# Second block of a transformer step: attention output in tiles of its own, two buffers for the S5 output matrix, gate tiles on a pair of banks, sums moved from GpSimd to VectorE

## Chip, cores and metric

One of the eight cores of a Trainium2 chip runs the kernel. Its engines are TensorE (PE in the rows, its weight loads PEld), VectorE (DVE), ScalarE (ACT), GpSimd (POOL) and SyncE (SP), which here issues DMAs. The metric is the device time of one execution in microseconds; lower is better.

## What is computed

The reference is two blocks in a row over 1024 tokens of 1024 columns. The first (differential attention, a gated delta rule, mixture of experts) and the last part of the second (output matrix, feed-forward) are not touched. What the change touches is the middle of the second block:

```python
h = _rms(x, norm1_g[l])
proj = h @ w_in[l]
u, q, k, v, qi, ki, wi, gates = jnp.split(proj, IN_SPLITS, axis=-1)
y_ssm = _s5_branch(u, A_re[l], ...)
...
```

`_s5_branch` is a state-space layer: 32 groups with 64 complex states each, scanned over time, then gelu and a gated linear unit (glu). The other branch is attention in blocks of 128 queries, in which each query sees only its 256 best keys by an index score (top-k). Both results go through a projection to 1024 columns, are multiplied by a sigmoid gate of their own (the 2048 columns `gates`) and added.

## The kernel before

Products have float32 accuracy: each operand is split into a high half, rounded to a format that TensorE takes in one pass, and a low half, and three matmuls (high by high, high by low, low by high) make one product (`K.mm3`). ACT makes the high half with a copy, another engine the low one by subtracting (`K.split`, L65 high and L66 low; for weights L75 `wh` and L76 `wl`, there on the engine in `K.sub`, which is GpSimd from the selection on).

The order of instructions on each engine is set by the scheduler of the tile framework, which takes the program's order and its own estimate of times; so a change in one place moves instructions in others. Tiles of one name share a ring of buffers. PSUM has the rings `lg` (two buffers of two banks), `tp` (two of one), `pj` and `po` (one each).

`stage_attn` is written in this order: norm of the input (`stage_norm2`, L1634 to L1650); index scores and queries; `select` for pairs of query blocks, a binary search for the top-k threshold (L1760 to L1846: count what lies above a threshold, one half on DVE and one on ACT, L1767, then one-element operations such as L1785), which ends in the mask `madd` (L1846); `attend` for the blocks 0 to 7; eight units of S5 (`s5_states`, `s5_out`), one beside each of the eight pieces of attend 6 and 7; 16 gate tiles of two halves each; `attn_branch` for the first 512 tokens (c=0) and for the others (c=1); `glu`; `merge`.

- `attend`: scores into `lg`, add of the mask with the maximum (L1867), exponential on ACT (L1870), reciprocal (L1872), scaling (L1876 on DVE from block 6 on, L1874 on POOL before), transposes into `tp` (L1883), split into `aph` and `apl` (L65, L66), product with V into `po`. Its queries are split by `stack` (L1665 on ACT, L1666 `aq`).
- `s5_states`: a matmul with `s5wi` into `lg`, products with cosines and sines (L1558 to L1560), a sum on POOL (L1561), four scans (L1563), the same back (L1565 on POOL, L1566, L1567), a sum (L1570). `s5_out` multiplies by `s5m` and `s5wo` and ends in gelu (L1585).
- `gate_tile` projects 128 gate columns in two halves of 24 matmuls of 128x512 through `pj` and takes a tanh (L1920). `u_tile` and `gate_tile` fill PE between the other parts.
- `attn_branch` loads the attention output `yatd` from DRAM (L1938), splits it into a part of the tile that held the block's input (`K.hh[:, 4:8]`), so after the gates of those columns have read it, multiplies by the projection, and applies the gate (L1950).
- `merge` adds the two branches (L2010 product with the gate, L2011 sum, L2012 and L2013 the split of the result).

Of the kernel before, what the change touches and what calls it, by code (L numbers as in the profile page):

```python
# [1530 lines left out]
def s5_states(K, wk, i, e):  # L1531


    nc = K.nc
    V, P = nc.vector, nc.gpsimd
    lo, hi = slice(0, 64), slice(64, 128)
    T = [128, 4, 128]
    g0 = 4 * i
    gs = slice(g0, g0 + 4)
    wi, wo, u = (wk.tile(T, F32, name="s5" + n, bufs=b) for n, b in (("wi", 2), ("wo", 1), ("u", 2)))  # L1540
    m = wk.tile([128, 4, 240], F32, name="s5m", bufs=2)
    cs = wk.tile([128, 4, 256], F32, name="s5cs", bufs=2)
    nc.sync.dma_start(wi, K.s5i[:, gs])
    nc.sync.dma_start(u, K.uTd[:, :, gs].rearrange("t p g c -> (t p) g c"))
    p0 = K.s5p[:, gs]
    nc.sync.dma_start(cs, bass.AP(tensor=p0.tensor, offset=p0.offset, ap=[[0, 2], [32 * 256, 64], [1, 1024]]))

    k0 = K.s5k[0:16, gs]
    nc.sync.dma_start(m.rearrange("p g x -> p (g x)")[:, 0:848],
                      bass.AP(tensor=k0.tensor, offset=k0.offset, ap=[[16, 8], [32 * 240, 16], [1, 848]]))  # L1550
    nc.sync.dma_start(wo, K.s5o[:, gs])
    co, si = cs[:, :, 0:128], cs[:, :, 128:256]
    e = e.rearrange("p (g c) -> p g c", g=4)
    for g in range(4):
        K.mm(e[:, g], wi[:, g], u[:, g], g == 0, True)

    a, r, z, c = (wk.tile(T, F32, name="s5" + n) for n in "arzc")
    V.tensor_mul(a, e, co)  # L1558
    V.tensor_mul(r[lo], e[hi], si[hi])
    V.scalar_tensor_tensor(r[hi], e[lo], -1.0, si[lo], op0=ALU.mult, op1=ALU.mult)  # L1560
    P.tensor_add(a, a, r)  # L1561
    for g in range(4):
        V.tensor_tensor_scan(z[:, g], K.rho[:, g0 + g:g0 + g + 1].to_broadcast([128, 128]), a[:, g], 0.0,  # L1563
                             op0=ALU.mult, op1=ALU.add)
    P.tensor_mul(c, z, co)  # L1565
    V.scalar_tensor_tensor(r[lo], z[hi], -1.0, si[hi], op0=ALU.mult, op1=ALU.mult)  # L1566
    V.tensor_mul(r[hi], z[lo], si[lo])  # L1567
    s = wk.tile([128, 4, 129], F32, name="s5s")
    P.memset(s[:, :, 0:1], 0.0)
    V.tensor_add(s[:, :, 1:129], c, r)  # L1570
    return m, u, wo, s
# [46 lines left out]
def stage_norm2(K, hp, ps):  # L1618

    nc, I = K.nc, K.I  # L1620
    K.hh = hp.tile([128, 8, L], F32R, name="hh")
    K.hl = hp.tile([128, 8, L], F32R, name="hl")
    K.rs1 = K.cst.tile([128, 8], F32, name="rs1")
    with ExitStack() as s:
        wk = K.pool(s, "n2w", 2, side="right")
        fg = wk.tile([128, D], F32, name="fg", bufs=1)
        gg = wk.tile([128, D], F32, name="gg", bufs=1)
        nc.sync.dma_start(fg, I["final_g"].rearrange("(a n) -> a n", a=1).to_broadcast([128, D]))
        nc.sync.dma_start(gg, I["norm1_g_2"].to_broadcast([128, D]))
        nc.gpsimd.tensor_mul(gg, gg, fg)  # L1630
        for t in range(8):
            ts = slice(t * 128, (t + 1) * 128)
            x = wk.tile([128, D], F32, name="x", bufs=4)
            nc.sync.dma_start(x, K.xacc[ts])  # L1634
            ss = wk.tile([128, 4], F32, name="ss")
            xf = wk.tile([128, D], F32, name="xf", bufs=3)
            (nc.gpsimd if t % 2 else nc.vector).tensor_mul(xf, x, fg)
            jk = wk.tile([128, D], BF, name="jk", bufs=1)
            nc.scalar.activation(jk, x, AF.Square, accum_out=ss[:, 0:1])
            nc.scalar.activation(jk, xf, AF.Square, accum_out=ss[:, 1:2])  # L1640
            r1 = K.rs1[:, t:t + 1]
            K.rstd(wk, r1, ss[:, 0:1], 1, 1, 1.0 / D)
            nc.vector.tensor_scalar(ss[:, 1:2], ss[:, 1:2], r1, r1, op0=ALU.mult, op1=ALU.mult)
            K.rstd(wk, ss[:, 2:3], ss[:, 1:2], 1, 1, 1.0 / D)
            nc.vector.tensor_mul(ss[:, 3:4], ss[:, 2:3], r1)
            nc.vector.scalar_tensor_tensor(xf, x, ss[:, 3:4], gg, op0=ALU.mult, op1=ALU.mult)
            for k0 in (0, 4):
                tp = ps.tile([128, 4, 128], F32, name="tp")
                for k in range(4):
                    nc.tensor.transpose(tp[:, k], xf[:, (k0 + k) * 128:(k0 + k + 1) * 128], K.ident)  # L1650
                K.split(K.hh[:, k0:k0 + 4, ts], K.hl[:, k0:k0 + 4, ts], tp)
# [197 lines left out]
def attend(K, wk, ps, b):  # L1849
# [3 lines left out]
    qt = wk.tile([128, 4, 128], F32, name="aqt")  # L1853
    nc.sync.dma_start(qt, K.qsd[b])
    qs = wk.tile([128, 2, 4, 128], F32R, name="aq", bufs=1)
    stack(K, qs, qt, nc.gpsimd.tensor_sub)
    for hp in range(2):
        po = ps.tile([128, 2, 2, 128], F32, name="po", bufs=1)
        for pp in range(2):
# [49 lines left out]
        nc.sync.dma_start(K.uTd[7 - t, :, f * 8:f * 8 + 8].rearrange("p g c -> g p c"), o[:, t])  # L1909


def gate_tile(K, wk, ps, f):

    nc = K.nc
    w = hcols(K, 1476 + f * 128, 128)
    o = wk.tile([128, L], F32, name="uo")
    for c in range(2):
        cs = slice(c * 512, (c + 1) * 512)
        q = proj_T(K, ps, w, 0, 128, c * 512, 512)
        nc.scalar.activation(o[:, cs], q, AF.Tanh, scale=0.5)  # L1920
    nc.sync.dma_start(K.sgt[f], o)

# [5 lines left out]
    yield q[:, 512:1024]  # L1928


def attn_branch(K, wk, gk, tag, ps, c):

    nc = K.nc
    cs = slice(c * 512, (c + 1) * 512)
    h, l = K.hh[:, 4:8, cs], K.hl[:, 4:8, cs]
    for k0 in (0, 2):
        r = wk.tile([128, 2, 512], F32, name=tag)
        nc.sync.dma_start(r, K.yatd[:, k0:k0 + 2, cs])  # L1938
        K.split(h[:, k0:k0 + 2], l[:, k0:k0 + 2], r)
    for f0 in (4, 6, 0, 2) if c else range(0, 8, 2):  # L1940
        if c == 0 or f0 < 4:
            K.wpa[f0] = K.wblock(K.I["w_proj_attn_2"][0], f0 * 128, 256)
        hs, ls = K.wpa[f0]
        g = gk.tile([128, 2, 512], F32, name=tag if c == 0 else "g", bufs=2 + 2 * c)
        nc.sync.dma_start(g, K.sgt[8 + f0:10 + f0, :, cs].rearrange("f p n -> p f n"))
        for i, q in enumerate((pair if c else narrow)(ps)):
            m = slice(i * 128, (i + 1) * 128)
            for k in range(4):
                K.mm3(q, (hs[k][:, m], ls[k][:, m]), (h[:, k], l[:, k]), k == 0, k == 3)
            nc.vector.scalar_tensor_tensor(g[:, i], g[:, i], 1.0, q, op0=ALU.add, op1=ALU.mult)  # L1950
        nc.sync.dma_start(K.mad[f0:f0 + 2, :, cs].rearrange("f p n -> p f n"), g)
# [42 lines left out]
def merge(K, wk, ps, y):  # L1994

    nc = K.nc
    A, B = K.hh, K.hl
    for f0 in range(0, 8, 2):
        hs, ls = K.wblock(K.I["w_proj_ssm_2"][0], f0 * 128, 256)
        for f in range(f0, f0 + 2):  # L2000
            g = wk.tile([128, L], F32, name="g", bufs=4)
            a = wk.tile([128, L], F32, name="ma")
            nc.sync.dma_start(g, K.sgt[f])
            nc.sync.dma_start(a, K.mad[f])
            m = slice((f - f0) * 128, (f - f0 + 1) * 128)
            for c, q in enumerate(pair(ps)):
                cs = slice(c * 512, (c + 1) * 512)
                for k in range(4):
                    K.mm3(q, (hs[k][:, m], ls[k][:, m]), (y[:, 0, k, cs], y[:, 1, k, cs]), k == 0, k == 3)
                nc.vector.scalar_tensor_tensor(g[:, cs], g[:, cs], 1.0, q, op0=ALU.add, op1=ALU.mult)  # L2010
                (nc.gpsimd if f < 7 else nc.vector).tensor_add(g[:, cs], g[:, cs], a[:, cs])  # L2011
                nc.scalar.activation(A[:, f, cs], g[:, cs], AF.Copy, scale=0.5)  # L2012
                nc.vector.scalar_tensor_tensor(B[:, f, cs], g[:, cs], 0.5, A[:, f, cs].bitcast(F32), op0=ALU.mult,  # L2013
                                               op1=ALU.subtract)


def stage_attn(K, hp, ew, dr):
# [8 lines left out]
    with ExitStack() as s:  # L2026
# [9 lines left out]
        with ExitStack() as s1:  # L2036
# [19 lines left out]
            w = hcols(K, 512, 512)  # L2056
            for t in range(8):
                q_tile(K, wk, ps, w, t)
        K.sub = nc.gpsimd.tensor_sub
        K.wh = wh  # L2060
        ps = Tags(pl, pj=pj, po=K.pool(s, "b3o", 1, PSUM))
        K.pjb = 1
# [14 lines left out]
        with ExitStack() as sw:  # L2077
# [5 lines left out]
            for _ in chain(attend(K, wk, ps, 6), attend(K, wk, ps, 7)):  # L2083
                next(units)
            next(units)
        for f in list(range(8, 16)) + list(range(8)):
            gate_tile(K, fk, ps, f)
        K.wpa = {}
        attn_branch(K, fk, fk, "uo", ps, 0)
        sa.close()  # L2090
        sr.close()
        bk = K.pool(s, "brw", 2)
# [1 line left out]
        with ExitStack() as sy:  # L2094
            yp = K.pool(sy, "yap", 1, side="right")
            ya = yp.tile([128, 2, 4, L], F32R, name="ya")
            with ExitStack() as sg:
                gk = K.pool(sg, "glw", 2)
                attn_branch(K, bk, bk, "ma", ps, 1)
                glu(K, bk, gk, ps, ya)  # L2100
            merge(K, bk, ps, ya)
        K.wh = w5
        K.w5 = out2_units(K, range(4))
    K.pjb = None
    K.sub = nc.vector.tensor_sub

def out2_units(K, us):
    wv = K.I["w_out_2"][0].rearrange("(k p) n -> p k n", p=128)
# [402 lines left out]
```

## Time and profile before

| | us |
|---|---|
| median of 3 runs | 3227.82 |
| lowest, highest run | 3227.03, 3231.82 |
| profiled execution, its own time | 3231.41 |
| its span | 3229.7 |

The stages of the profiled execution that the text speaks of:

| stage | us from the span's start |
|---|---|
| norm, scores, queries | 1776.6 to 1870 |
| selection, with attend 0 to 5 | 1870 to 2189.8 |
| attend 6 and 7, S5, the last gates, attention c=0 | 2189.8 to 2384.1 |
| attention c=1 and glu | 2384.1 to 2432 |
| merge, start of the output matrix | 2432 to 2482.5 |

The page gives shares of the whole span. The table by stage and the waits inside a stage tell which engine ends it. A row of waits reads: who waited, for whom, us in total, times, longest.

### The profile page before, as it was taken

Reading aid. Unit: us, or ns where it says so; the run is one execution under the profiler, and the core shown is the slowest. Engines: PE = TensorE matmul, PEld = TensorE weight load, DVE = VectorE, ACT = ScalarE, POOL = GpSimd, SP = SyncE. Lnnn points to the kernel's source line nnn. Section 1 sums busy time; section 2 is a strip of 40 time slices with the busy share of each in tenths; the row PEclk is TensorE's granted clock in tenths of the full one; section 3 lists DMA queues with packets and bytes.
Section 4 is the critical chain, followed back from the end, with each engine's and each line's share of the span. In section 5 each row is a group of like instructions: output and inputs, shape, how many; then the busy total and the mean of one; then the engine's idle time right before and its main releaser. Section 6 shows DMA issues by size and latency. Waiting matters only on the chain. (4 is left out here: it accounts for less than half of the span.)

```text
span 3229.7 us, 45092 instructions
## 1 busy us (share of the span) xinstructions
PE 2900.7 (90%) x15573; PEld 2387.0 (74%) x15573; DVE 2445.2 (76%) x4878; ACT 1656.9 (51%) x3161; POOL 804.9 (25%) x719
## 2 busy tenths in 40 slices
PE   3987999889897969999999699897698999999999
PEld 1655888778786748887777577776576788888787
DVE  6787665998886499999988599985567586555675
ACT  4433455365665228887776577663433243333343
POOL 4376111154554521111101324332225000000000
PEclk7988999889998979999999799999899999999999
DMA  5545665535324559999997223224575323333732
GB/s 204 150 144 170 192 182 175 151 112 152 105 86 144 176 189 379 382 398 366 370 372 249 73 66 90 65 70 128 136 248 177 123 72 103 109 109 105 290 111 101
DMA packets 370783, 567.04 MB, mean 176 GB/s; under 512 B 73075, under 2 KB 208104, under 8 KB 370554
## 3 DMA queue, kind: packets, MB, share of 16 engines
q1 hardware_dynamic: 365946, 547.37, 50.1%
q0 software_dynamic: 4608, 16.78, 2.2%
q8 instruction: 123, 2.02, 0.3%
q14 instruction: 106, 0.87, 0.1%
HBM read 446.12 MB, written 117.95 MB: 175 GB/s over the span
## 5 line engine op out<-in xcount | busy, mean ns | idle before, releaser
L1221 DVE TENSOR_TENSOR wl<-wraw,wh 128x1024 fp32r<-128x1024 f32 x384 | 446.9, 1217 | 10.9 <-ACT wh L1220 10.4
L1220 ACT ACTIVATE wh<-wraw 128x1024 fp32r<-128x1024 f32 x384 | 391.6, 1060 | 80.4 <-PE pu L57 42.6
L57 PE MATMUL pj<-hh,wh 128*128 128x512 f32 (+1 forms) x768 | 300.9, 392 | 17.6 <-ACT uo L1920 8.5
L57 PE MATMUL pj<-hh,wl 128*128 128x512 f32 (+1 forms) x768 | 295.7, 387 | 1.5 <-POOL wl L76 1.5
L57 PE MATMUL pj<-hl,wh 128*128 128x512 f32 (+1 forms) x768 | 295.9, 386 | 0.0
L57 PEld LDWEIGHTS pj<-hh,wh 128*128 128x128 f32 x768 | 148.3, 193 | 53.2 <-ACT uo L1920 11.7
L57 PEld LDWEIGHTS pj<-hh,wl 128*128 128x128 f32 x768 | 147.8, 193 | 35.4 <-issue 6.8
L57 PE MATMUL pj<-wh,hh 128*128 128x512 f32 (+1 forms) x400 | 159.8, 400 | 12.8 <-DVE g L2010 8.2
L57 PEld LDWEIGHTS pj<-hl,wh 128*128 128x128 f32 x768 | 148.2, 193 | 28.7 <-issue 3.8
L76 POOL TENSOR_TENSOR wl<-wraw,wh 128x1024 fp32r<-128x1024 f32 (+1 forms) x56 | 130.6, 2334 | 147.7 <-ACT wh L75 147.5
L704 ACT ACTIVATE E<-sc,dst 128x512 f32<-128x512 f32 (+1 forms) x192 | 117.7, 618 | 87.0 <-DVE dst L703 80.1
L57 PE MATMUL pj<-wh,hl 128*128 128x512 f32 (+1 forms) x400 | 159.1, 398 | 0.0
L57 PE MATMUL pj<-wl,hh 128*128 128x512 f32 (+1 forms) x400 | 158.5, 396 | 0.0
L75 ACT ACTIVATE wh<-wraw 128x1024 fp32r<-128x1024 f32 (+2 forms) x88 | 88.8, 1014 | 79.9 <-DMA wraw<-in_w_in_dram 28.9
L1284 POOL DMA_INDIRECT xacc<-ye,ix x16 | 37.1, 2318 | 326.4 <-DVE ye L1283 240.9
L703 DVE TENSOR_REDUCE dst<-sc 128x1 f32<-128x512 f32 (+1 forms) x192 | 109.2, 593 | 10.7 <-PE sc L57 9.8
L718 POOL TENSOR_TENSOR E<-E,dst 128x512 f32<-128x512 f32 (+1 forms) x96 | 94.5, 1011 | 69.8 <-DVE dst L715 48.2
L57 PE MATMUL pu<-wl,xh 128*128 128x512 f32 x256 | 101.6, 398 | 11.2 <-DVE wl L1221 11.0
L1767 ACT ACTIVATE bja<-isc,bca 128x384 bf16<-128x384 f32 (+2 forms) x96 | 79.3, 827 | 52.2 <-DVE bca L1785 25.7
L57 PE MATMUL sc<-da_ka,da_qh 128*128 128x512 f32 (+1 forms) x192 | 85.9, 452 | 22.0 <-ACT E L704 20.6
L57 PE MATMUL pg<-wl,xh 128*128 128x512 f32 x256 | 102.7, 401 | 0.2 <-DVE wl L1221 0.2
L57 PE MATMUL py<-wl,hh 128*128 128x512 f32 x256 | 100.4, 396 | 0.3 <-DVE wl L1221 0.3
(833 smaller groups left out, 8663.0 us busy)
## 6 DMA issues: line engine op xcount, KB each, us to landing
wraw<-in_w_gate_dram SPq DMA_DIRECT2D x64, 1024.0 KB
wraw<-in_w_up_dram SPq DMA_DIRECT2D x64, 1024.0 KB
wraw<-in_w_down_dram SPq DMA_DIRECT2D x64, 1024.0 KB
wraw<-in_w_in_dram SPq DMA_DIRECT2D x52, 512.0 KB
raw<-hsd SPq DMA_DIRECT2D x38, 512.0 KB
mw<-in_w_mod_dram SPq DMA_DIRECT2D x64, 256.0 KB
raw<-in_w_ffn_gate_dram SPq DMA_DIRECT2D x22, 512.0 KB
raw<-in_w_ffn_up_dram SPq DMA_DIRECT2D x22, 512.0 KB
```

Of the source, the lines that this page charges most:

```text
L57: self.nc.tensor.matmul(out, lhsT, rhs, start=start, stop=stop, skip_group_check=True)
L75: nc.scalar.activation(h, raw, AF.Copy)
L76: self.sub(l, raw, h.bitcast(F32))
L703: nc.vector.tensor_reduce(mn[:, i, j:j + 1], p[:, :n], axis=AX.X, op=ALU.min)
L704: nc.scalar.activation(e[:, c0:c0 + n], p[:, :n], AF.Exp, bias=mn[:, i, j:j + 1], scale=-1.0, accum_out=ls[:, i, j:j + 1])
L718: nc.gpsimd.tensor_mul(e1, e1, sc[:, 1, j:j + 1].to_broadcast([128, n]))
L1220: nc.scalar.activation(h, raw[:, k], AF.Copy)
L1221: nc.vector.tensor_sub(l, raw[:, k], h.bitcast(F32))
L1284: nc.gpsimd.indirect_dma_start(out=K.xacc, out_offset=bass.IndirectOffsetOnAxis(ap=idx[e][:, :1], axis=0), in_=ye, in_offset=None, compute ...
L1767: self.K.nc.scalar.activation(jk[:, :self.n], self.x, AF.Sign, bias=cand, scale=-1.0, accum_out=cnt)
```

## The change

1. `s5wo` has two buffers in place of one.
2. In `s5_states` the sum L1561 and the product L1565 go from GpSimd to VectorE; `c` shares the buffer of `a`.
3. In the norm the odd products (L1637) go from GpSimd to VectorE.
4. In `attend` the subtraction for `aq` goes from GpSimd to VectorE, and so do the weights' low halves (`K.sub` stays VectorE throughout).
5. In `merge` all 16 sums are on VectorE; 14 were on GpSimd.
6. The split of the attention output stands in a function of its own. For c=0 it is written ahead of the gates and goes into tiles of its own.
7. Gate tiles after the tenth, and attention c=0, take their two halves from the pair of rings `lg` and `tp`, not from `pj`.

```diff
-    wi, wo, u = (wk.tile(T, F32, name="s5" + n, bufs=b) for n, b in (("wi", 2), ("wo", 1), ("u", 2)))
+    wi, wo, u = (wk.tile(T, F32, name="s5" + n, bufs=b) for n, b in (("wi", 2), ("wo", 2), ("u", 2)))
...
-    a, r, z, c = (wk.tile(T, F32, name="s5" + n) for n in "arzc")
+    a, r, z = (wk.tile(T, F32, name="s5" + n) for n in "arz")
...
-    P.tensor_add(a, a, r)
+    V.tensor_add(a, a, r)
...
-    P.tensor_mul(c, z, co)
+    c = wk.tile(T, F32, name="s5c", tag="s5a")
+    V.tensor_mul(c, z, co)
...
-            (nc.gpsimd if t % 2 else nc.vector).tensor_mul(xf, x, fg)
+            nc.vector.tensor_mul(xf, x, fg)
...
-    stack(K, qs, qt, nc.gpsimd.tensor_sub)
+    stack(K, qs, qt, nc.vector.tensor_sub)
...
-def gate_tile(K, wk, ps, f):
+def gate_tile(K, wk, ps, f, two):
...
-    for c in range(2):
+    for c, q in enumerate((pair if two else narrow)(ps)):
         cs = slice(c * 512, (c + 1) * 512)
-        q = proj_T(K, ps, w, 0, 128, c * 512, 512)
+        for k in range(8):
+            K.mm3(q, (w[0][k], w[1][k]), (K.hh[:, k, cs], K.hl[:, k, cs]), k == 0, k == 7)
...
+def attn_parts(K, wk, tag, c, h, l):
+
+    for k0 in (0, 2):
+        r = wk.tile([128, 2, 512], F32, name=tag)
+        K.nc.sync.dma_start(r, K.yatd[:, k0:k0 + 2, c * 512:(c + 1) * 512])
+        K.split(h[:, k0:k0 + 2], l[:, k0:k0 + 2], r)
...
-        for i, q in enumerate((pair if c else narrow)(ps)):
+        for i, q in enumerate(pair(ps)):
...
-                (nc.gpsimd if f < 7 else nc.vector).tensor_add(g[:, cs], g[:, cs], a[:, cs])
+                nc.vector.tensor_add(g[:, cs], g[:, cs], a[:, cs])
...
-        K.sub = nc.gpsimd.tensor_sub
...
-        for f in list(range(8, 16)) + list(range(8)):
-            gate_tile(K, fk, ps, f)
+        ap = K.pool(sr, "abr", 2, side="right")
+        h, l = (ap.tile([128, 4, 512], F32R, name="ab" + n, bufs=1) for n in "hl")
+        attn_parts(K, ap, "abi", 0, h, l)
+        for i, f in enumerate(list(range(8, 16)) + list(range(8))):
+            gate_tile(K, fk, ps, f, i > 9)
         K.wpa = {}
-        attn_branch(K, fk, fk, "uo", ps, 0)
+        attn_branch(K, fk, "uo", ps, 0, h, l)
```

What the scheduler makes of it stands in the order of the instructions on an engine. Names there are out<-in, with the line; lines of the changed kernel are 1 to 5 higher. ACT in the middle of S5, before: `s5y` is the output of a unit, `as` an exponential, `uo<-pj` a half of a gate, `hh<-uo` the split of the attention output, `wh` a weight's high half.

```order
L1585 ACT_TABLE_LOAD
L1585 ACTIVATE s5y<-lg 128x512
L1870 ACT_TABLE_LOAD
L1870 ACTIVATE as,ast<-as,ast 128x1024
L65 ACTIVATE hh<-uo 128x2x512
L1893 ACTIVATE aol<-po 64x512
L75 ACTIVATE wh<-wraw 128x1024
L65 ACTIVATE hh<-uo 128x2x512
L1920 ACTIVATE uo<-pj 128x512
L1870 ACTIVATE as,ast<-as,ast 128x1024 x2
```

ACT from the last cycles of S5 on, now:

```order
L1871 ACT_TABLE_LOAD
L1871 ACTIVATE as,ast<-as,ast 128x1024 x2
L1586 ACT_TABLE_LOAD
L1586 ACTIVATE s5y<-lg 128x512
L65 ACTIVATE aph<-tp 128x512 x4
L1894 ACTIVATE aol<-po 64x512
L1922 ACTIVATE uo<-tp 128x512
L1586 ACTIVATE s5y<-lg 128x512
L75 ACTIVATE wh<-wraw 128x1024
L1922 ACTIVATE uo<-lg 128x512
```

Gates and the split of the attention output have left the cycles; twelve gate halves follow behind attend 7, and the split (`abh<-abi`) stands between those. On PE the gate matmuls move in the same way: 24 halves stood ahead of the first S5 unit and 8 between the units; now 20 stand ahead and 12 behind the seventh.

DVE in the second unit of S5, now; before, the two operations into `s5a` (the sum) and `s5c` stood on POOL:

```order
L1561 TENSOR_TENSOR s5a<-s5a,s5r 128x512
L1868 ISA as,ast<-lg,madd 128x896
L1868 ISA ast 128x1
L1563 SCALAR_TENSOR_TENSOR s5z<-rho,s5a 128x128 x4
L1870 TENSOR_SCALAR ast<-ast 128x1
L66 TENSOR_TENSOR apl<-tp,aph 128x512
L1897 TENSOR_TENSOR ay<-po,aol 64x256 x2
L1566 TENSOR_TENSOR s5c<-s5z,s5cs 128x512
L1567 SCALAR_TENSOR_TENSOR s5r<-s5z,s5cs 64x512
```

A unit's chain now stands on DVE as a whole, with pieces of attend between its steps.

DVE at the end of the selection of blocks 6 and 7, before (`bjv`, `bwv`, `se`, `sc` are steps of the search's end, `madd` is the mask):

```order
L1760 TENSOR_SCALAR bjv,bgv<-isc,bcv 128x1024
L1843 SCALAR_TENSOR_TENSOR sc<-onesr,se 128x896
L1818 TENSOR_SCALAR bwv<-bgv 128x1
L1844 SCALAR_TENSOR_TENSOR se<-sc,bwa,se 128x896
L1896 TENSOR_TENSOR ay<-po,aol 64x256 x2
L1845 SCALAR_TENSOR_TENSOR se<-isc,bca,se 128x896
L1846 TENSOR_SCALAR madd<-se 128x896
```

And the same place now:

```order
L1761 TENSOR_SCALAR bjv,bgv<-isc,bcv 128x1024
L1844 SCALAR_TENSOR_TENSOR sc<-onesr,se 128x896
L76 TENSOR_TENSOR wl<-wraw,wh 128x1024
L1819 TENSOR_SCALAR bwv<-bgv 128x1
L1845 SCALAR_TENSOR_TENSOR se<-sc,bwa,se 128x896
L1846 SCALAR_TENSOR_TENSOR se<-isc,bca,se 128x896
L1847 TENSOR_SCALAR madd<-se 128x896
```

A weight's low half stands in front of the last steps of the selection. Between the first search step and the last mask, 16 such and 14 `aq` rows have come to DVE.

## Rows read from the trace of the kernel before

**Rows 1.** The page, part 1: busy time, share of the span and instructions of each engine.

```profile
PE 2900.7 (90%) x15573; PEld 2387.0 (74%) x15573; DVE 2445.2 (76%) x4878; ACT 1656.9 (51%) x3161; POOL 804.9 (25%) x719
```

**Rows 2.** Stages: us; busy PE, PEld, DVE, ACT, POOL (instructions); clock, DMA, GB/s.

```profile
1870.00:2189.80 319.80, 293.95 (x1462) 243.01 (x1460) 300.88 (x1003) 214.33 (x454) 118.97 (x94) 0.98 0.24 72
...
2189.80:2384.10 194.30, 149.08 (x828) 128.25 (x827) 113.14 (x202) 75.39 (x108) 45.68 (x34) 0.90 0.54 155
...
2432.00:2482.50 50.50, 42.34 (x187) 34.72 (x187) 39.28 (x35) 17.35 (x24) 39.22 (x21) 0.96 0.59 208
```

**Rows 3.** Waits, PE and DVE, 2189.8 to 2384.1: us in total, times, longest.

```profile
PE lg L57 <- issue: 20.4, 1, 20.4
...
PE lg L57 <- DMA s5wo<-s5o: 12.9, 3, 9.8
...
DVE ast L1872 <- ACT as L1870: 21.6, 10, 4.9
...
DVE apl L66 <- ACT aph L65: 14.6, 6, 6.7
```

**Rows 4.** Timeline at the stall: start, us, engine, what, [idle before it].

```profile
2315.52 0.37 SPq L1938 DMA_DIRECT2D uo<-yatd  x1
...
2329.05 1.06 ACT L65 ACTIVATE hh<-uo 128x1024 fp32r<-128x1024 f32 x1 [20.43 <-DMA uo<-yatd]
```

**Rows 5.** Windows of one S5 cycle and two stretches, columns as rows 2.

```profile
2256.80:2274.70 17.90, 17.55 (x106) 15.12 (x105) 13.33 (x26) 9.67 (x14) 5.51 (x4) 1.00 0.58 140
...
2225.00:2250.00 25.00, 15.11 (x77) 13.24 (x78) 12.13 (x24) 8.55 (x15) 5.51 (x4) 0.80 0.51 153
...
2325.00:2350.00 25.00, 13.58 (x61) 11.94 (x62) 16.75 (x30) 9.76 (x14) 5.37 (x4) 0.66 0.53 159
```

**Rows 6.** Chain of waits, 2432 to 2600: start, us, what.

```profile
2517.20 16.19 PE pj L57 x70
```

**Rows 7.** DVE groups, 2189.8 to 2384.1: busy us, mean ns | idle before.

```profile
L1563 DVE TENSOR_TENSOR_SCAN s5z<-rho,s5a 128x128 f32<-128x128 f32 x32 | 10.9, 405 | 2.1 <-POOL s5a L1561 2.0
...
L1867 DVE CUSTOM_DVE_ANT_0 as<-lg,madd 128x1024 f32<-128x1024 f32 x8 | 9.7, 1218 | 1.3 <-PE lg L57 1.3
...
L1876 DVE TENSOR_SCALAR as<-as,ast 128x1024 f32<-128x1024 f32 x8 | 6.0, 749 | 0.2
...
L66 DVE TENSOR_TENSOR apl<-tp,aph 128x512 fp32r<-128x512 f32 x28 | 18.8, 687 | 14.8 <-ACT aph L65 14.6
...
L1560 DVE SCALAR_TENSOR_TENSOR s5r<-lg,s5cs 64x512 f32<-64x512 f32 x8 | 5.5, 683 | 0.1
...
L66 DVE TENSOR_TENSOR hl<-uo,hh 128x1024 fp32r<-128x1024 f32 x2 | 2.5, 1225 | 21.4 <-ACT hh L65 21.4
```

**Rows 8.** A POOL group in the same stretch.

```profile
L1565 POOL TENSOR_TENSOR s5c<-s5z,s5cs 128x512 f32<-128x512 f32 x8 | 13.1, 1636 | 16.8 <-issue 13.8 <-DVE s5z L1563 3.0
```

**Rows 9.** Groups, one line's durations and a wait of the selection, 1870 to 2189.8.

```profile
L76 POOL TENSOR_TENSOR wl<-wraw,wh 128x1024 fp32r<-128x1024 f32 x17 | 41.7, 2452 | 49.8 <-ACT wh L75 49.6
...
L1666 POOL TENSOR_TENSOR aq<-aqt,aq 64x512 fp32r<-64x512 f32 x14 | 18.2, 1298 | 13.0 <-ACT aq L1665 7.4 <-issue 4.1 <-POOL as L1874 0.7
...
L1785 DVE SCALAR_TENSOR_TENSOR bcv<-bcv,bmv 128x1 uint32<-128x1 uint32 x90 | 25.1, 279 | 0.4
...
L1785 DVE SCALAR_TENSOR_TENSOR bca<-bca,bma 128x1 uint32<-128x1 uint32 x89 | 23.9, 268 | 0.3
...
L1785 DVE SCALAR_TENSOR_TENSOR bca<-bca,bma x89: 144/155/2131, 1871.8 to 2165.3; 128x1 uint32<-128x1 uint32 x89
...
DVE bma L1773 <- ACT bja L1767: 10.0, 9, 2.4
```

**Rows 10.** Merge, 2432 to 2482.5: a wait of ACT, a wait of PE.

```profile
ACT hh L2012 <- POOL g L2011: 18.2, 11, 4.7
...
PE pj L57 <- DVE g L2010: 8.2, 1, 8.2
```

**Rows 11.** Timeline of the norm's start, 1776 to 1800.

```profile
1793.13 2.33 POOL L1637 TENSOR_TENSOR xf<-x,fg 128x1024 f32<-128x1024 f32 x1
```

More of the change, by code (lines that the diff above doesn't have):

```diff
@@ L1928, in wide, with attn_branch @@
     yield q[:, 512:1024]
-def attn_branch(K, wk, gk, tag, ps, c):
+def attn_parts(K, wk, tag, c, h, l):
[3 more added lines that the diff above has]
+        K.split(h[:, k0:k0 + 2], l[:, k0:k0 + 2], r)
+def attn_branch(K, gk, tag, ps, c, h, l):
     nc = K.nc
     cs = slice(c * 512, (c + 1) * 512)
[L1935 to L1939, printed above, removed]
     for f0 in (4, 6, 0, 2) if c else range(0, 8, 2):
@@ L2098, in stage_attn @@
                 gk = K.pool(sg, "glw", 2)
-                attn_branch(K, bk, bk, "ma", ps, 1)
+                h, l = K.hh[:, 4:8, 512:1024], K.hl[:, 4:8, 512:1024]
+                attn_parts(K, bk, "ma", 1, h, l)
+                attn_branch(K, bk, "ma", ps, 1, h, l)
                 glu(K, bk, gk, ps, ya)
@@ L2104, in stage_attn @@
     K.pjb = None
-    K.sub = nc.vector.tensor_sub
 def out2_units(K, us):
```

## The prediction

> **What bounds the kernel now.** I read the page's busy shares first: TensorE (PE) is busy for 90% of the span, VectorE (DVE) for 76%, GpSimd (POOL) for 25% [rows 1]. So a gain must come out of PE's idle time, and I looked for it by stage. In the table by stage [rows 2] the reader is to see three regimes. In the selection (1870 to 2189.8 us) DVE is busy for 300.9 of 319.8 us: VectorE sets the end, with 18.9 us to spare. In the S5 stretch (2189.8 to 2384.1) no engine is full: PE 149.1 of 194.3 us. In the merge (2432 to 2482.5) PE is busy for 42.3 of 50.5 us and POOL, which adds there, for 39.2. Then the waits of the S5 stretch [rows 3]: PE stands 20.4 us once, and 12.9 us for the matrix `s5wo`. The timeline says what the 20.4 us are [rows 4]: SP issues the load of the attention output into `uo` at 2315.5, ScalarE (ACT) waits 20.43 us for it in front of the split, DVE waits for ACT, PE for DVE. Last, single S5 cycles between these stalls [rows 5]: from 2256.8 to 2274.7 PE is busy for 17.55 of 17.9 us, because gate projections fill it, while DVE is busy for 13.3.
>
> **The parts with one answer.** A second buffer for `s5wo` takes away the 12.9 us of waits [rows 3]. Own tiles for the attention output take the ACT wait out of the S5 stretch [rows 4]: the loads stand early on SP's queue, and the split stands behind gates on ACT. SP's queue has them behind the S5 output's writes and the glu loads; their data is needed only after twelve gate halves (some 65 us later), so I cost that at nothing; the cover is those gates, and without it the load to landing, up to 13.5 us (2315.5 to 2329.0), would stand before attention. The pair of banks for late gate tiles saves a bank's hand-over; the waits for `uo` at gates are not among the long ones of [rows 3], so nothing.
>
> **S5 stretch.** The shorter waits are not all that changes here: the order does. Before, 8 gate halves and all of the attention's first half stand between the S5 units; now 20 gate halves stand ahead of the first unit, seven units with their attention pieces follow with no gate between, and then 12 halves (288 matmuls) and attention c=0 (96). I rebuild the stretch. One cycle on DVE [rows 7]: eight elementwise operations of 0.683 us, since both sums come from POOL (5.5), four scans (10.9/8 = 1.4), two reductions (2.4), two scalings (1.5), four `apl` subtractions (2.7), small ones some 1.2 (an estimate): 14.7 us; with the next block's `aq` and edges I take 15.4. The product L1565 took 1.64 us on POOL [rows 8]; with the sum L1561 taken alike and 0.683 each on DVE, the unit's chain is shorter by some 1.9 us and DVE's work longer by 1.4. To this come DVE's waits for ACT: 21.6 + 14.6 = 36.2 us over eight units before [rows 3], 4.5 in each, of which part was the stalls and PE's fill. They lie between 0 and 4.5; I take 2.1, as DVE must still wait for the exponential of the second parity and for the split of the transposes on ACT. Cycle: 17.5 us, near the 17.9 of the undisturbed one of [rows 5], where it was PE that was full. The stretch: 3.7 us from the last mask to the first unit (by the order one scaling and two `apl` stand between, 0.75 and 1.4 us by [rows 7], and 1.5 of waits), six cycles to the last unit with nothing beside it 105, 3 until PE starts on gates, 384 matmuls at 16.19/70 = 0.231 us [rows 6] 88.7, and 4 at the seams: 204.4 against 194.3, **+10.1**. The matmuls that were cover for S5 now stand behind it: what the 33 us of stalls give back, they take.
>
> **Selection.** Sixteen weights' low halves and fourteen `aq` subtractions come to the engine that sets the end here. On DVE the first is the 1.225 us of a subtraction of that shape, the second the 0.683 of a 64x512 one [rows 7]: 19.6 + 9.6 = 29.2 us added. Taken off: one-element operations of the search stretch behind POOL. Most take 0.155 us; all 179 take 25.1 + 23.9 = 49.0 [rows 9], so 21.3 us are held time. The moved ones are 41.7 + 18.2 = 59.9 us of POOL's 119.0 [rows 2, 9], half; the longest holds (above 2 us) fit only the 2.45 us low halves, and larger operations are held too, not counted in the 21.3. Between 10.7 (half) and 30 I take 19. Net 10, of which 6 go into idle time such as the 10.0 us of waits for ACT's half of the search [rows 9]: **+4**, between -9 and +12.
>
> The Trainium skill (SBUF — State Buffer, section "Who interferes with whom") says that a DVE operation with two SBUF inputs and a GpSimd operation that reads SBUF exclude each other wholly, the later one waiting for the other's end; the 1.225 us subtractions now meet the softmax multiplications that stay on POOL. By it they would cost some 3 us more (an estimate: 30 operations, POOL busy with the rest for 59 of 319.8 us, half an operation's wait each). The held rows agree with the rule; the bound of +12 has room for it.
>
> **Merge and the rest.** Of the merge's 16 additions 14 stand on POOL, and ACT waits 18.2 us for them [rows 10]; on DVE one takes 0.68, and DVE, busy 39.3 of 50.5 us [rows 2] with held operations, gets 9.6 us more work and loses the holding. PE waits for the end of it for 8.2 us [rows 10]: **-4**, between -8 and +2. In the second norm the POOL product of 2.33 us [rows 11] leaves the start: **-2**, between -2.3 and 0. Weight halves in the glu stage: **-1.5**, between -3 and 0.
>
> Sum: +10.1 + 4 - 4 - 2 - 1.5 = +6.6. The profiled execution took 3231.4 us, 3.6 above the median of the runs, 3227.8; by it the sum gives 3238, by the median 3234.4. I forecast **3235 us**. About 0.2% (6.5 us) is what a measurement can tell from no change.
>
> **The rivals.**
> A, faster: with no gates in its way PE answers at once, and S5 runs at DVE's own work, 15.4 us a cycle: -12.6 us; and the selection gains what POOL's holding cost (-4 rather than +4). 6.6 - 12.6 - 8 = -14: 3214. It decides when DVE's waits per cycle fall under 1 us. For it: DVE idles 4.6 us in a cycle in which PE was full [rows 5]. Against it: a table load of ACT before and after each S5 output stays.
> B, slower: DVE takes its work in order, and a low half waits for ACT's high half; on POOL nobody stood behind it. With 1 us of waiting at each of sixteen, before the search steps behind them, +16: 3251. For it: POOL waited 49.6 us for ACT's `wh` over 17 of them [rows 9]. Against: the order puts them some operations after their `wh`.
> C, slower: TensorE's clock. The stretches 2225 to 2250 and 2325 to 2350, where PE had stood idle, show granted clocks of 0.80 and 0.66; a filled cycle 1.00 [rows 5]. Clock 0.5 is the lower level, 1.2 GHz. Seven cycles without fill leave PE waiting in each; if each has its scores and transposes at the lower level, some 3 us (12 of 0.231) more on the cycle's path, +18: 3253.
> [...]
> D, no change: S5 cycles of 16.5 and a selection at zero, -6 and -4: 3225 to 3231. The end is the same from other places.
>
> **How the numbers follow.** Forecast, with an own spread of some 7 us, 0.42; A 0.30; B 0.09; C 0.10; D 0.09. Of the forecast's 0.42, 0.23 are over +0.2%, 0.17 within, 0.02 faster. Faster: 0.28 of A and 0.02, 0.30. Within: 0.17, 0.02 of A, 0.07 of D, 0.26. Slower: 0.23 + 0.09 + 0.10 + 0.02 = 0.44. For the range I leave out A's lower end (S5 at its floor, selection at -9 and merge at -8 would be some 3205) and B and C together: 3209 to 3255.
>
> **What would show it.** Right: PE without a wait of over 5 us on `s5wo` or the split; the first unit's `s5a` about 4 us after the last mask and then one each 17 to 18 us; DVE waits on ACT of about 2 us a cycle; after the seventh unit some 90 us of PE without a gap; selection longer by a few us with no POOL low half; merge some 4 us shorter. Wrong: cycles of 15.5 us or less (A), a row "wl waits for wh" of over 10 us on DVE in the selection (B), a granted clock under 0.8 through the S5 cycles (C), or gate matmuls between the units after all. The forecast falls if the stretch from the last mask to attention c=1 is under 192 us.

## The result, and the profile after

The changed kernel takes 3248.14 us (median of 4 runs, 3243.37 to 3250.91) against 3227.84: ratio 1.0053, 95% interval 1.0042 to 1.0065. It is slower, by 20 us and not by the 7 of the forecast; the range holds it.

Part 1 of its page, which answers to [rows 1]: GpSimd's work has shrunk from 804.9 to 642.7 us, PE's busy share is the same.

```profile
PE 2915.5 (90%) x15573; PEld 2394.1 (74%) x15573; DVE 2471.6 (76%) x4964; ACT 1655.7 (51%) x3159; POOL 642.7 (20%) x633
```

The stages after, columns as [rows 2]: the selection, the start of S5 with its first cycle, the next five cycles, gates with attention c=0, the merge.

```profile
1870.00:2186.40 316.40, 281.33 (x1409) 231.27 (x1408) 303.61 (x1030) 211.91 (x451) 61.05 (x62) 0.97 0.24 72
2186.40:2225.00 38.60, 21.63 (x96) 18.70 (x96) 18.28 (x41) 10.76 (x17) 0.10 (x1) 0.64 0.42 110
2225.00:2311.50 86.50, 61.25 (x343) 51.61 (x342) 70.73 (x142) 42.88 (x63) 0.76 (x6) 0.84 0.46 117
2311.50:2410.00 98.50, 95.76 (x440) 79.33 (x439) 40.27 (x57) 26.36 (x37) 0.11 (x1) 0.98 0.61 195
...
2455.00:2502.00 47.00, 47.00 (x208) 38.75 (x207) 40.32 (x57) 20.64 (x27) 0.00 (x0) 1.00 0.67 224
```

Selection and merge are shorter than in [rows 2] (316.4 for 319.8 us; PE without a gap through the 47 us of the merge). The stretch from the last mask to the end of attention c=0, in bounds like those of [rows 2], is 223.6 us for 194.3. Its start with the first cycle has a granted clock of 0.64 and PE busy for 21.6 of 38.6 us, the next five cycles 0.84 and 61.3 of 86.5; then PE is busy for 95.8 of 98.5 us, with the matmuls that stood between the units before. The waits of PE in that stretch (columns as [rows 3]):

```profile
PE lg L57 <- DVE ast L1868: 16.4, 8, 4.3
PE tp L1884 <- DVE ast L1873: 16.1, 1, 16.1
PE lg L57 <- DVE s5r L1560: 14.7, 7, 9.8
PE lg L57 <- DMA s5m<-s5k: 4.5, 1, 4.5
```

The two long ones of [rows 3] are gone, as forecast. The 16.1 us end with the selection: gates no longer fill PE there to the end. Then come small waits of every cycle, PE for DVE, and one at the start, which the timeline shows (columns as [rows 4]):

```profile
2185.50 0.56 SPq L1546 DMA_DIRECT2D s5cs<-s5p  x1
...
2200.63 0.69 DVE L1558 TENSOR_TENSOR s5a<-lg,s5cs 128x512 f32<-128x512 f32 x1 [10.64 <-DMA s5cs<-s5p]
...
2202.87 0.76 PE L57 MATMUL lg<-kh,aq 128*128 128x512 f32 x1 [9.76 <-DVE s5r L1560]
```

The first unit's `s5cs` is issued when DVE has read the last of the selection's scores, whose memory S5's buffers take by the program (a wait of SP in the changed kernel):

```profile
SPq L1546 <- DVE se L1846: 8.9, 1, 8.9
```

It lands 15.1 us later; DVE waits 10.64 us and PE, behind it, 9.76. The same load was there before, as two rows of that kernel's timeline show, from 2188.80 to 2204.88, but DVE waited 2.07 us only, and PE had gate matmuls. From the last mask to the first unit's `s5a` it is 15.1 us before and 14.2 now, and from 14.2 to 16.3 in all kernels of this document: the change did not make this wait, it took away the work that stood over it.

```profile
2188.80 0.56 SPq L1546 DMA_DIRECT2D s5cs<-s5p  x1
...
2204.88 0.69 DVE L1558 TENSOR_TENSOR s5a<-lg,s5cs 128x512 f32<-128x512 f32 x1 [2.07 <-DMA s5cs<-s5p]
```

In the selection the longest hold of [rows 9], in the timeline of the kernel before, ends where the low half ends that had begun just before it:

```profile
2079.56 2.39 POOL L76 TENSOR_TENSOR wl<-wraw,wh 128x1024 fp32r<-128x1024 f32 x1
...
2079.83 2.13 DVE L1785 SCALAR_TENSOR_TENSOR bca<-bca,bma 128x1 uint32<-128x1 uint32 x1
```

Now the 179 one-element operations take 36.1 us, not 49.0, beside the low halves on their own engine:

```profile
L76 DVE TENSOR_TENSOR wl<-wraw,wh 128x1024 fp32r<-128x1024 f32 x16 | 19.5, 1218 | 0.1
L1786 DVE SCALAR_TENSOR_TENSOR bca<-bca,bma 128x1 uint32<-128x1 uint32 x89 | 19.2, 216 | 0.1
...
L1786 DVE SCALAR_TENSOR_TENSOR bcv<-bcv,bmv 128x1 uint32<-128x1 uint32 x90 | 16.9, 188 | 0.3
```

### The profile page after: what moved, and what is told of

It reads as the page before. It is cut to its first block, busy times and chain, and to the rows that moved or that the text cites. A ratio compares the mean times of both kernels' runs of the same rounds, so it can differ in the third digit from the quotient of the medians.

```text
span 3249.2 us, 45057 instructions
## 1 busy us (share of the span) xinstructions
PE 2915.5 (90%) x15573; PEld 2394.1 (74%) x15573; DVE 2471.6 (76%) x4964; ACT 1655.7 (51%) x3159; POOL 642.7 (20%) x633
## 5 line engine op out<-in xcount | busy, mean ns | idle before, releaser
L1221 DVE TENSOR_TENSOR wl<-wraw,wh 128x1024 fp32r<-128x1024 f32 x384 | 447.1, 1219 | 11.2 <-ACT wh L1220 10.7
L57 PE MATMUL pj<-hh,wh 128*128 128x512 f32 (+1 forms) x640 | 248.1, 388 | 10.9 <-ACT cvraw L331 5.9
L57 PE MATMUL pj<-hh,wl 128*128 128x512 f32 (+1 forms) x640 | 246.2, 386 | 1.5 <-POOL wl L76 1.5
L57 PE MATMUL pj<-hl,wh 128*128 128x512 f32 (+1 forms) x640 | 245.9, 385 | 0.0
L57 PEld LDWEIGHTS pj<-hh,wh 128*128 128x128 f32 x640 | 124.0, 194 | 39.2 <-ACT cvraw L331 7.4
L57 PEld LDWEIGHTS pj<-hh,wl 128*128 128x128 f32 x640 | 123.9, 194 | 29.8 <-issue 6.8
L57 PEld LDWEIGHTS pj<-hl,wh 128*128 128x128 f32 x640 | 123.9, 194 | 24.6 <-issue 4.3
L76 DVE TENSOR_TENSOR wl<-wraw,wh 128x1024 fp32r<-128x1024 f32 (+1 forms) x68 | 83.0, 1223 | 55.3 <-ACT wh L75 50.7
L57 PE MATMUL sc<-da_ka,da_qh 128*128 128x512 f32 (+1 forms) x192 | 85.6, 450 | 19.4 <-ACT E L704 18.1
```

Of the source, the lines that this page charges most:

```text
L57: self.nc.tensor.matmul(out, lhsT, rhs, start=start, stop=stop, skip_group_check=True)
L76: self.sub(l, raw, h.bitcast(F32))
L1221: nc.vector.tensor_sub(l, raw[:, k], h.bitcast(F32))
```

## The experiments

Each kernel is compared with the kernel before on the same chip. From the timeline of one profile of each come three lengths: the **selection** (start of the norm's last transpose to the end of the last mask), the **S5 part** (from there to the end of attention c=1) and the **merge part** (from there to the end of the merge's last high half on ACT; the rest of glu lies in it).

| kernel | us | ratio (95%) | selection | S5 part | merge part |
|---|---|---|---|---|---|
| before | 3227.8 | 1 | 355.8 | 216.6 | 77.9 |
| changed | 3248.1 | 1.0053 (1.0042 to 1.0065) | 351.4 | 246.0 | 71.2 |
| e1 gates through pj | 3235.2 | 1.0008 (0.9998 to 1.0017) | 352.3 | 234.0 | 70.8 |
| e2 before, gates in pairs | 3287.3 | 1.0171 (1.0154 to 1.0188) | 355.4 | 265.9 | 77.5 |
| e3 e1, split in the old place | 3221.0 | 0.9969 (0.9957 to 0.9981) | 348.5 | 224.7 | 70.9 |
| e4 e1, one `s5wo` | 3235.5 | 1.0015 (1.0005 to 1.0024) | 350.0 | 233.1 | 71.2 |
| e5 e1, no split | 3214.1 | 0.9950 (0.9931 to 0.9969) | 349.8 | 214.8 | 71.1 |
| e6 e3, other slots | 3223.6 | 0.9979 (0.9969 to 0.9990) | 349.7 | 224.8 | 71.4 |
| e7 e3, low halves on GpSimd | 3244.4 | 1.0045 (1.0030 to 1.0059) | 357.5 | 224.9 | 77.9 |
| e8 e3, S5 sums on GpSimd | 3228.0 | 0.9995 (0.9981 to 1.0009) | 350.1 | 228.9 | 70.8 |
| e9 e3, attention through pj | 3214.0 | 0.9955 (0.9942 to 0.9968) | 349.4 | 213.6 | 72.5 |
| e10 before, low halves on VectorE | 3216.1 | 0.9958 (0.9945 to 0.9971) | 351.4 | 212.2 | 71.9 |
| e11 e9, loads by GpSimd | 3201.7 | 0.9909 (0.9896 to 0.9922) | 349.5 | 206.7 | 71.6 |
| e12 changed, fewer matmuls | 3226.7 | 0.9986 (0.9974 to 0.9997) | 349.5 | 225.5 | 71.0 |

The median of the kernel before was 3230.4 to 3231.3 us in the experiments' groups, so ratios compare across groups better than times.

**e1** undoes the pair of banks for late gates:

```diff
-            gate_tile(K, fk, ps, f, i > 9)
+            gate_tile(K, fk, ps, f, False)
```

> The changed kernel with one edit undone: every gate tile takes its halves from the one bank pj, as before; attention c=0 keeps the pair, all else stays as changed. In the order the gate matmuls stand between the S5 units again. Theory (cover): the pair of banks for the late gate tiles is what moved them behind S5, and the loss is matmul work that covers nothing. Then the stretch from the last mask to the end of attention c=0 falls from 223.6 us to 175 to 190, and the time to 3200 to 3215 us, below both kernels. Rival 1 (the sums that went to VectorE lengthen the S5 cycles whatever PE does): cycles stay at 17 us or more with gates in them and come to 20, the time stays above 3235. Rival 2 (the 10.6 us wait for the first unit's s5cs and its clock are the loss): it stays, 3235 to 3245.

Measured: 12 us less in the S5 part, 13 in all, where the theory had 33 to 48. At 3235.2 us the time is at the lower edge of what both rivals said. The cycles, 17.3 to 23.9 us and 20.5 in the mean, are those of rival 1, and the first unit still starts 14.5 us behind the mask, as rival 2 has it; so this run alone decides against neither. (e9 does, which keeps the sums on VectorE and the first wait and has a shorter S5 part than the kernel before, and for the sums e8.) The gates do stand between the units again, but two new waits of PE stand at the last unit and behind it:

```profile
PE lg L57 <- DVE s5s L1571: 17.5, 1, 17.5
PE lg L57 <- ACT abh L65: 13.0, 1, 13.0
```

The second is the split of the attention output into its own tiles. SP issues those loads last of all, behind the writes of the last S5 output (its timeline):

```profile
2363.41 3.65 SPq L1589 DMA_DIRECT2D ysd<-s5y  x8
...
2367.65 1.59 SPq L1937 DMA_DIRECT2D abi<-yatd  x2
```

In the program the pool of those tiles is opened when S5's is closed, on the same side, so its tiles take S5's memory and cannot be filled while units run. So "ahead of the gates" in the program's text is behind S5 in time. That became the second theory, for e3 and e5.

**e2** makes that edit alone, in the kernel before:

```diff
-        for f in list(range(8, 16)) + list(range(8)):
-            gate_tile(K, fk, ps, f)
+        for i, f in enumerate(list(range(8, 16)) + list(range(8))):
+            gate_tile(K, fk, ps, f, i > 9)
```

> The kernel before with this one edit of the change alone: gate tiles after the tenth take the pair of rings lg and tp. Theory (cover): the gates go behind S5 here too; the split of the attention output waits behind them, the s5wo buffer is single: 3245 to 3265 us, S5 cycles of 17 to 19 us with no gate between them. Rival 1 (sums on VectorE): 3222 to 3234, as no sum has moved. Rival 2 (first unit's loads): about 3238.

Measured: 1.7% slower, the S5 part 49.3 us longer, more than any theory gave. One edit, of no arithmetic at all, moves the gates behind S5: the rings `lg` and `tp` serve scores, transposes and S5, and in the order the late gates now stand behind these. In the changed kernel the same edit costs 12.0 us of the S5 part (against e1); why it costs four times as much alone was not taken apart.

**e3** puts the split back where it was, behind the gates, with e1's gates:

```diff
-        ap = K.pool(sr, "abr", 2, side="right")
-        h, l = (ap.tile([128, 4, 512], F32R, name="ab" + n, bufs=1) for n in "hl")
-        attn_parts(K, ap, "abi", 0, h, l)
+        h, l = K.hh[:, 4:8, 0:512], K.hl[:, 4:8, 0:512]
+        attn_parts(K, fk, "uo", 0, h, l)
```

> As e1, and the attention output of c=0 is split into the columns of the block input again, through the slots uo behind the gates. Theory (cover): against e1 this measures the own tiles: the load behind the slot brings back a wait of up to 20 us, or moves attention c=0 between the S5 units as more cover; 3205 to 3230. If own tiles are worth nothing, as e1 within 4 us.

Measured: 9.3 us less in the S5 part than e1, 14 in all, and already below the kernel before. The wait for the load behind the slot is back (waits of ACT), yet attention c=0 now stands between the last units.

```profile
ACT hh L65 <- DMA uo<-yatd: 27.2, 2, 19.7
```

**e4** gives e1 one `s5wo` buffer (`("wo", 2)` to `("wo", 1)`).

> As e1 with one buffer for s5wo. The waits of the kernel before for it were 12.9 us in all. If they are on the path, 6 to 13 us above e1; if something else is late in their place, within 4 us of e1.

Measured: no difference. In e4's trace PE's waits for `s5wo` are back, and longer than the 12.9 us of [rows 3]; the wait at the last unit, 17.5 us in e1, is shorter in their place:

```profile
PE lg L57 <- DMA s5wo<-s5o: 19.4, 5, 8.4
...
PE lg L57 <- DVE s5s L1571: 9.6, 1, 9.6
```

**e5** leaves the split out of e1, and attention c=0 reads other data:

```diff
-        h, l = (ap.tile([128, 4, 512], F32R, name="ab" + n, bufs=1) for n in "hl")
-        attn_parts(K, ap, "abi", 0, h, l)
+        h, l = K.hh[:, 0:4, 0:512], K.hl[:, 0:4, 0:512]
```

> As e1 (late gates through pj), and the split of the attention output for c=0 is left out with its tiles and its load: attention c=0 multiplies columns of the block's input instead (that product is not the attention's). Theory (own tiles stand in memory that S5 releases last, so the split and the product come behind S5): the waits of 17.5 and 13.0 us of e1 go, PE has attention c=0 between the last S5 units, 20 to 30 us below e1: 3205 to 3215. Rival (S5's own pace on VectorE holds the end): within 8 us of e1, 3227 to 3243.

Measured: 21 us below e1, 19.2 of them in the S5 part: what waits for the own tiles costs that much. (Load, split and tiles go together here; neither the memory nor the place of the loads on SP's queue was tried by itself.)

**e6** gives e3's loads the slots of `aqt`, in four pieces of 128x512:

```diff
-        attn_parts(K, fk, "uo", 0, h, l)
+        for k in range(4):
+            r = wk.tile([128, 4, 128], F32, name="aqt")
+            nc.sync.dma_start(r, K.yatd[:, k, 0:512].rearrange("p (a b) -> p a b", a=4))
+            K.split(h[:, k], l[:, k], r.rearrange("p a b -> p (a b)"))
```

> As e3 (gates through pj, split into the columns of the block's input), but the loads go through the slots of aqt, idle after the last attend, in four pieces, not through uo, which gates hold. Theory: the wait of 19.7 us of ACT for the load of e3 and PE's 16.2 us behind it go, as the loads can be issued as soon as the last block's queries are read: 3205 to 3214. Rival (something else is late in its place, such as the last unit of S5 or its loads): within 6 us of e3's 3221.

Measured: the rival, no gain. The first two pieces came in time, the last two did not (its timeline):

```profile
2283.52 14.44 SPq L1589 DMA_DIRECT2D ysd<-s5y  x8
...
2303.80 2.38 SPq L2096 DMA_DIRECT2D aqt<-yatd  x2
...
2320.92 1.31 ACT L65 ACTIVATE hh<-aqt 128x512 fp32r<-128x512 f32 x2 [28.23 <-DMA aqt<-yatd]
```

SP stands 14.44 us over the eight writes of an S5 output, issues the next units' loads, then these two; they land 17 us later, and ACT, in order, stands 28.23 us in front of them while the last scores and the S5 output wait behind it.

**e7** puts low halves and `aq` back on GpSimd in e3 (`K.sub = nc.gpsimd.tensor_sub` again, `stack(K, qs, qt, nc.gpsimd.tensor_sub)`).

> As e3, with the weights' low halves and the aq subtraction on GpSimd as before. Theory (their move paid in the selection, as its one-element operations are no longer held behind GpSimd): the selection grows by 3 to 9 us and the time to 3224 to 3231. Rival (the prediction's +4 for the selection): 3 to 5 us faster than e3, 3216 to 3218.

Measured: 23 us slower, far beyond the forecast: 9.0 us of it in the selection, 7.0 in the merge, none in the S5 part; the rest lies outside the three, where such profiles also differ by some us between themselves. The one-element operations are held again as in [rows 9]:

```profile
L76 POOL TENSOR_TENSOR wl<-wraw,wh 128x1024 fp32r<-128x1024 f32 x17 | 41.7, 2453 | 49.2 <-ACT wh L75 49.0
...
L1786 DVE SCALAR_TENSOR_TENSOR bcv<-bcv,bmv 128x1 uint32<-128x1 uint32 x90 | 26.9, 299 | 0.4
...
L1786 DVE SCALAR_TENSOR_TENSOR bca<-bca,bma 128x1 uint32<-128x1 uint32 x89 | 24.0, 270 | 0.3
```

And in the merge, where the additions are on VectorE in this kernel too, the additions and the splits are held (first e7, then the changed kernel):

```profile
L76 POOL TENSOR_TENSOR wl<-wraw,wh 128x1024 fp32r<-128x1024 f32 x9 | 22.7, 2521 | 49.8 <-ACT wh L75 49.8
...
L2016 DVE TENSOR_TENSOR g<-g,ma 128x512 f32<-128x512 f32 x16 | 16.7, 1051 | 1.3 <-DMA ma<-mad 1.2
L2018 DVE SCALAR_TENSOR_TENSOR hl<-g,hh 128x512 fp32r<-128x512 f32 x15 | 15.2, 1015 | 2.0 <-ACT hh L2017 1.3
```

```profile
L2016 DVE TENSOR_TENSOR g<-g,ma 128x512 f32<-128x512 f32 x16 | 11.0, 686 | 0.4 <-DMA ma<-mad 0.4
...
L2018 DVE SCALAR_TENSOR_TENSOR hl<-g,hh 128x512 fp32r<-128x512 f32 x14 | 9.5, 685 | 0.0
```

**e8** puts the S5 sums back on GpSimd in e3 (`P.tensor_add(a, a, r)`, `P.tensor_mul(c, z, co)`).

> As e3, with the two S5 sums on GpSimd as before. Rival 1 of the first group (the sums lengthen the cycles on VectorE): 8 us or more faster than e3. Theory (their move shortens each unit's chain by 1.9 us and adds 1.4 us of VectorE work, so nothing is left): within 5 us of e3, 3216 to 3226.

Measured: 7 us slower, 4.2 in the S5 part. On VectorE the sums are a gain of about that size (its runs lie from 3221.0 to 3236.2 us, so the size is rough); the theory's bound of 5 us was too low, and the rival has the sign wrong. Whether the unit's chain or the new order makes the gain is open: PE's longest wait for `s5y` is 29.0 us here and 16.2 in e3.

**e9** is e3 with attention c=0 through `pj` (`enumerate((pair if c else narrow)(ps))`).

> As e3, and attention c=0 also takes its halves from the one bank pj, as before; of the change this leaves the second s5wo buffer and all that went from GpSimd to VectorE. In the order four pieces of attention c=0 stand between the last S5 units instead of two. e3's stretch from the last mask to the end of attention c=1 was 224.7 us, 8.1 longer than before. Theory (cover: what stands between the units is what counts, and the pair put attention behind them too): the stretch falls to 205 to 214, the time to 3206 to 3215. Rival (attention c=0 is no cover, the stall of e3 holds the end): within 5 us of e3's 3221.

Measured: as the theory said, the S5 part 213.6 us.

**e10** is the kernel before with low halves and `aq` on VectorE alone:

```diff
-    stack(K, qs, qt, nc.gpsimd.tensor_sub)
+    stack(K, qs, qt, nc.vector.tensor_sub)
...
-        K.sub = nc.gpsimd.tensor_sub
```

> The kernel before with one edit: weights' low halves and the aq subtraction on VectorE. Theory (the selection gains by it, e7 against e3 read the other way round): the selection from the end of the norm to the last mask falls from 355.8 us to 348 to 352, the part from the end of attention c=1 to the last split of the merge from 77.9 to about 71, the stretch between stays at 217 within 4: 3214 to 3222. Rival (the prediction's +4 in the selection): 3229 to 3236 less what the merge gives, 3225 to 3229.

Measured: 0.42% faster, selection 4.4 us and merge part 6.0 us shorter, and 4.4 us off the S5 part, just over the 4 that the expectation allowed, with the merge's additions still on GpSimd. So the merge's gain belongs to the low halves; the additions by themselves bring nothing that can be seen.

**e11** is e9 with e6's loads, issued by GpSimd (`nc.gpsimd.dma_start(r, ...)`).

> As e9, with the attention output loaded in four pieces through the idle slots of aqt, issued by GpSimd and not by SP. In e6 SP stood 14.4 us over the writes of an S5 output before it issued two of these loads, and ACT stood 28.2 us for them. Theory (the place on SP's queue is what makes the load late): that wait falls under 12 us and the time to 3 to 15 us below e9. Rival (the load takes its 13 to 17 us wherever it is issued and ACT stands for it in order): within 3 us of e9, or slower.

Measured: 12 us below e9, 0.9% below the kernel before, the fastest of all. The load that stood on SP until 2303.8 in e6 and took 17 us is issued as soon as DVE has read its slot, and lands in 6 (its timeline on GpSimd, then on ACT):

```profile
2288.65 1.16 POOL L2096 DMA_DIRECT2D aqt<-yatd  x2 [12.31 <-DVE hl L66]
```

```profile
2294.81 0.63 ACT L65 ACTIVATE hh<-aqt 128x512 fp32r<-128x512 f32 x1 [1.57 <-DMA aqt<-yatd]
2296.28 0.63 ACT L65 ACTIVATE hh<-aqt 128x512 fp32r<-128x512 f32 x1 [0.84 <-DMA aqt<-yatd]
```

PE's wait for `s5y`, behind ACT, falls with it (waits of PE, e9 and then e11):

```profile
PE lg L57 <- ACT s5y L1586: 16.9, 1, 16.9
```

```profile
PE lg L57 <- ACT s5y L1586: 1.1, 1, 1.1
```

e11 has the change without the three edits that lose, and with this load, which the change did not have. The slots alone brought nothing on SP's queue in e3 (e6); e9 with them on that queue was not run.

**e12** leaves most matmuls of the late gates out of the changed kernel (`for k in range(1 if two else 8)`).

> The changed kernel, and of each half of the six late gate tiles only 3 of 24 matmuls are left (the gates' sums are not whole): 12 x 21 = 252 matmuls fewer, everything else in its place. At 0.231 us they are 58.2 us of matmul. Theory (behind S5 nothing runs beside them, they stand on the path in full): 50 to 60 us below the changed kernel, 3188 to 3198. Rival (they hide other waits, such as the loads of gates and weights for attention, which come up when they go): 15 to 40 us below, 3208 to 3233.

Measured: the rival, 21.5 us for 58.2 us of matmul. When they go, loads and the split that they hid come up:

```profile
PE lg L57 <- ACT abh L65: 15.0, 1, 15.0
...
PE tp L57 <- ACT wh L75: 6.0, 2, 4.8
```

## Why the prediction was right, and where it was not

The direction was right and so was its core: the S5 part ends later because work that covered it left it, by the pairs of banks for the larger part and by the own tiles. The steps:

- **Stalls that go.** Right in the trace: neither long wait of [rows 3] is left. But the second `s5wo` buffer was worth nothing in e1's order (e4). That the late gates cover the split was right: without most of their matmuls PE waits 15.0 us for it (e12), where the prediction had up to 13.5. Between gates the own tiles cost 9.3 us (e1 against e3), which it put at nothing.
- **The cycles.** The forecast had 17.5 us; the five cycles from 2224.8 to 2311.5 take 17.3 each. There is some luck in that: DVE is busy for 14.1 us and idle for 3.2 in each, for 15.4 and 2.1 in the forecast. PE starts on gates 3.6 us after the last of these units (forecast 3), and the 88.7 us of matmul with 4 of seams took 94.7 (2315.2 to 2409.9).
- **The step that failed is the start of the stretch**, "3.7 us from the last mask to the first unit" and six equal cycles. It is 14.2 us to the first unit, as the load needs 15.1 from its issue and its issue hangs on the selection's last read; the first cycle then takes 24.1. That is 17 of the 19 us that the stretch was too short. The order shows no load; [rows 5]'s kind of window shows only what PE did over it. It stood in the timeline of the kernel before, hidden under gates that the forecast itself had moved away: I costed the cover's loss in matmuls, and not in what else it covered.
- **The selection**, forecast +4, measured -3.4 from 1870 us to the last mask. DVE's busy time rose by 2.7 us where 29.3 were added (19.5 of low halves and 9.8 of `aq`), so 26.6 us of holding went, where I took 19 (my bounds were 10.7 and 30): 12.9 of it from the one-element operations, the rest from larger ones. Idle time fell by 6.1, as taken. The Trainium skill (SBUF — State Buffer, "Who interferes with whom") has the later of two such operations wait for the other's whole end; the two rows of 2079.56 and 2079.83 agree, and with the low halves back on GpSimd the holds are back (e7). The 3 us that the prediction worked out against the change are not seen: the 128x1024 subtractions on VectorE took 1.218 us for 1.225.
- **The merge and glu**, forecast -4 and -1.5, measured -6.7 together (the merge part), but for the wrong reason in the merge: it is the low halves (e7, e10), not the additions.
- **The norm's start**, forecast -2, cannot be told: its first transpose stood between 1797.0 and 1802.1 us in profiles of kernels with one and the same norm.
- **Rivals.** A did not come in the cycles, DVE's waits for PE and ACT stayed in them; its other half, a selection at -4, did. B fell: in the selection `wl` waits 0.1 us in all. C is there in part, granted clocks of 0.64 and 0.84 where PE waits (in e12 0.66 from 2300 to 2340 us); how much of the 12 us between e1 and the changed kernel is clock and how much is order was not tried apart.

So the 29.4 us of the S5 part come together thus, each by one kernel against the next: from before to e9 -3.0, attention c=0 in pairs +11.1 (e3), own tiles in S5's memory +9.3 (e1), late gates in pairs +12.0. Against them stand 4.4 us of selection and 6.7 of merge. These shares hold in this order of edits: alone, in the kernel before, the late gates in pairs cost 49.3 us (e2). The range held the time although the stretch was 19 us off, because the selection was 7.4 better than forecast; without that the time would stand at the range's upper end of 3255. This was luck.

## What to carry to other kernels

In a kernel ordered by a scheduler, giving filler work the buffers of the work that it fills can take the fill away: before a second bank is given, look whose bank it is, and look in the new order where the filler went. When cover moves, list all that it covered, loads too: in the trace of before, everything that was issued under it and landed under it. And undo a change of seven parts one by one: here three lost 32 us in the S5 part together, while the others left a version 0.45% faster than before (e9), and 0.9% with one load moved to another engine's queue (e11).

## What was not expected of the hardware

- Small VectorE operations of 0.155 us were held up to 2.1 us by single GpSimd subtractions of 2.45 us; taking these and `aq` off GpSimd gave back 26.6 us of the 29.3 that they cost on VectorE.
- SP took from 3.65 us (e1) to 16.1 us (e12) to issue the eight writes of one S5 output; in e6 two loads stood behind 14.44 us of them, while GpSimd's queue was free in e11 (17 us to land for 6).
- Waits can be worth nothing: 19.4 us of them (e4 against e1) changed the time by no more than the measurement tells; and work can be worth less than its length: 58.2 us of matmul on a nearly full PE gave 21.5 (e12).
